# Mixture-of-experts stage of a two-block model on one core: half-array products, transposes and sums put in runs

## Chip, cores and metric

The kernel runs on one core of a Trainium2 chip. The metric is the device time of one execution in microseconds (us), as the median of several runs.

## What is computed

Two model blocks follow each other. The change touches only the last stage of the second block, a hierarchical mixture of experts over 512 tokens of width 1024, in float32:

```python
for g in range(N_GROUPS):
    a = jnp.einsum('td,edf->tef', t, w_gate[g])
    b = jnp.einsum('td,edf->tef', t, w_up[g])
    m = jax.nn.silu(a) * b * combine[:, g, :, None]
    y = y + jnp.einsum('tef,efd->td', m, w_down[g])
```

There are 32 experts in all, each with 256 inner columns; `combine` is zero but for the two best experts of a token's best group. After the stage comes a residual addition and one RMS norm, and the kernel ends.

## The kernel before, in words

A routing step (before the stage) gives each expert a list of at most 64 rows (`CAP`); a list that is longer is finished in a loop at the very end (`further`), which runs zero times here. Each expert is handled on 64 columns of the array, two experts to a pair, so that the 128 partitions of a pair's result are 64 slots of one and 64 of the other.

- **Weights.** An expert's weights come as three pieces of 1 MB (`load_pieces`, issued on the queue of SP, six after each pair), into a ring of 17 tiles (`ew`, `mix`, `cb` in the trace). A tile is loaded again when the products that read it are done; SP waits for that in order.
- **Rows.** The tokens' rows are gathered from memory by POOL (`gather`, eight ahead; tile `hy`), turned on TensorE by four transposes into a bank `pt` (`expert_rows`, line 277), and written to `ex` by VectorE with the norm's gain (line 1906).
- **Inner products** (`expert_inner`, line 1920): 16 matmuls of an expert, 8 contraction steps k for two column halves f. Each uses one half of the array (128x64 weights, 256 columns), the two f side by side. A float32 matmul stands in the trace as two records. The result, in a bank `lin`, goes through ScalarE (Silu, line 1925) and VectorE (line 1926) to `em`; one transpose puts it into `pt`, and VectorE copies it to `emt` (line 1932).
- **Outer products** (`expert_steps`, line 1945): 8 matmuls of a pair, for two halves f of the contraction and two halves i of the 1024 outputs; the two experts of the pair use the two halves of the array side by side. Results stand in two banks `sc`. ScalarE writes their weighted high part and VectorE the low part, both to `ca` (lines 1951, 1952).
- **Sums** (line 1965): eight per pair, for four blocks c of 128 tokens and two halves i. Each is two full-array matmuls of 512 columns with a 0/1 matrix `esel` that puts slots back at their tokens; it lands in one bank, `o` or `bg` by turns, and VectorE adds it to `xrow` (line 1967).

The order around the change: the sums of a pair are a generator (`sums`), and the next pair's `expert_inner` takes a step of it at four places (`beside`): after k = 4, after the products, after the next expert's row transposes, and after the copy to `emt`. So one sum stands at each of eight places of a pair. The list order is only the starting point; a scheduler may move instructions on their engines, save those under `keep_in_program_order`. PSUM has eight banks, by name: two `lin`, two `sc`, two `pt`, one `o`, one `bg`.

```python
some = lambda: next(sums, None)
beside = (some, some, lambda: (rows(e), some()), some)
inner.append(self.expert_inner(ahead.pop(), piece(e), self.slot_rstd[:, e:e + 1], beside))
```

Of the kernel before, what the change touches and what calls it, by code (L numbers as in the profile page):

```python
# [11 lines left out]
F32 = mybir.dt.float32  # L12
# [6 lines left out]
P = 128  # L19
# [86 lines left out]
class Builder:  # L106
    def __init__(self, ctx, tc, a, out):
        self.tc, self.nc, self.a, self.out = tc, tc.nc, a, out
        pool = lambda name, bufs=1, **kw: ctx.enter_context(tc.tile_pool(name=name, bufs=bufs, **kw))
        self.cp = pool("const")  # L110
        self.sm = None
        self.ps = pool("psum", 8, space=bass.MemoryType.PSUM)
        self.uid = 0
        self.background = iter(())
        self.opened, self.seconds = {}, {}
        self.np, self.nw, self.ahead = None, S, 2
        self.turn, self.probs = True, 2
        self.meanwhile = iter(())

    def open(self, name, side="left"):  # L120
# [153 lines left out]

    def transpose(self, out, in_):
        k = in_.shape[0]
        self.nc.tensor.transpose(out, in_, self.ident[:k, :k])  # L277

    def rstd(self, acc, count, ones=None):

# [1626 lines left out]
                                     op=ALU.mult)  # L1907
        return x

    def expert_inner(self, x, pieces, r, beside=None):  # L1910


        nc = self.nc
        beside = beside or [lambda: None] * 4

        ps = self.psum()
        for k in range(KC):
            xk = x[:, P * (k % 4) + CAP * (k // 4):P * (k % 4) + CAP * (k // 4) + CAP]
            for f in range(2):
                nc.tensor.matmul(ps[CAP * f:CAP * f + CAP, :256], xk, pieces(512 * k + 256 * f, 256), start=k == 0,  # L1920
                                 stop=k == KC - 1, tile_position=(0, CAP * f))
            if k == KC // 2:
                beside[0]()
        m = self.t([P, P], F32, "em", 2)
        nc.scalar.activation(out=m, in_=ps[:, :P], func=AF.Silu, scale=r)
        nc.vector.scalar_tensor_tensor(out=m, in0=ps[:, P:2 * P], scalar=r, in1=m, op0=ALU.mult, op1=ALU.mult)
        beside[1]()
        beside[2]()
        pt = self.psum("pt")
        self.transpose(pt[:, :P], m)  # L1930
        mt = self.t([P, P], F32, "emt", 3)
        nc.vector.tensor_copy(mt, pt[:, :P])
        beside[3]()
        return mt

    def expert_steps(self, inner, pieces, y, token, weight):


        nc = self.nc
        n = CAP * len(inner)  # L1940
        o = [self.psum("sc") for _ in range(2)]
        for f in range(2):
            for i in range(2):
                for e, (mt, pc) in enumerate(zip(inner, pieces)):
                    nc.tensor.matmul(o[i][CAP * e:CAP * e + CAP], mt[:, CAP * f:CAP * f + CAP],  # L1945
                                     pc(4096 + 1024 * f + 512 * i, 512), start=f == 0, stop=f == 1,
                                     tile_position=(0, CAP * e))
        ys = []
        for i in range(2):
            yh, yl = y[:n, 2 * i], y[:n, 2 * i + 1]  # L1950
            nc.scalar.activation(out=yh, in_=o[i][:n], func=AF.Copy, scale=weight)
            nc.vector.scalar_tensor_tensor(out=yl, in0=o[i][:n], scalar=weight, in1=yh, op0=ALU.mult,
                                           op1=ALU.subtract)
            ys.append((yh, yl))

        sel = self.t([P, S], FR, "esel", 2)[:n]
        for i in range(2):
            nc.vector.tensor_scalar(out=sel[:, C * i:C * i + C], in0=self.rests[4 + i][:n], scalar1=token, scalar2=None,
                                    op0=ALU.is_equal)
        yield  # L1960
        for c in range(4):
            for i in range(2):
                ps = self.psum(("o", "bg")[i])
                for part in range(2):
                    nc.tensor.matmul(ps, sel[:, c * P:c * P + P], ys[i][part], start=part == 0, stop=part == 1)  # L1965
                acc = self.xrow[4 * i + c]
                nc.vector.tensor_tensor(out=acc, in0=acc, in1=ps, op=ALU.add)
                yield
# [81 lines left out]
    def moe(self):  # L2050
# [19 lines left out]

        def rows(e):

            if e + 1 < 32:
                ahead.append(self.expert_rows(gs[(e + 1) % GATHERED]))
            if e + GATHERED < 32:
                gather(e + GATHERED)

        def piece(e):
            return lambda c, n: self.pieces[3 * e + c // 2048][:, c % 2048:c % 2048 + n]

        for q in range(16):
            inner = []
            for e in (2 * q, 2 * q + 1):
                some = lambda: next(sums, None)
                beside = (some, some, lambda: (rows(e), some()), some)
                inner.append(self.expert_inner(ahead.pop(), piece(e), self.slot_rstd[:, e:e + 1], beside))
            if q == 15:

                self.tc.keep_in_program_order(
                    nc.scalar.activation(out=self.trstd[:, :1], in_=self.eps, func=AF.Sqrt))  # L2090
            sums = self.expert_steps(inner, [piece(2 * q), piece(2 * q + 1)], y, self.pair_token[:, q:q + 1],
                                     self.pair_weight[:, q:q + 1])
            next(sums)
            self.load_pieces(6)
        last = [self.last(c) for c in range(4)]
        for c in range(4):
            whole(itertools.islice(sums, 2))
            next(last[c])
            if c > 0:
                whole(last[c - 1])  # L2100
        whole(last[3])
        self.further(y)
        self.close("moe", "later", "inputs")

    def further(self, y):
# [4 lines left out]
        with self.tc.For_i(0, count, 1) as i:  # L2110
            e = nc.values_load(self.ov[0:1, bass.ds(i, 1)], engines=[mybir.EngineType.SP], min_val=0, max_val=31)
            sl = self.t([P, 4], F32, "osl", 1)
            nc.sync.dma_start(sl, self.table[bass.ds(i, 1)].rearrange("t p c -> p (t c)"))
            oi = self.t([P, 1], I32, "oid", 1)
            nc.vector.tensor_copy(oi, sl[:, 0:1])
            self.gather(g, oi)
            w = [self.t([P, 2048], F32, "ew", RING[0], self.rings[0][0]) for _ in range(3)]
            for k in range(3):
                nc.sync.dma_start(w[k], a["w_moe"][bass.ds(e, 1), :, 2048 * k:2048 * k + 2048].rearrange("e p c -> p (e c)"))
            piece = lambda c, n: w[c // 2048][:, c % 2048:c % 2048 + n]  # L2120
            inner = self.expert_inner(self.expert_rows(g), piece, sl[:, 3:4])
            whole(self.expert_steps([inner], [piece], y, sl[:CAP, 1:2], sl[:CAP, 2:3]))
            for c in range(4):
                whole(self.last(c))

# [216 lines left out]
```

## Time and profile before

| | |
|---|---|
| median of 3 runs (lowest to highest) | 2652.45 us (2650.92 to 2658.2) |
| the profiled execution's own time | 2654.92 us |
| its span, first to last instruction | 2653.1 us |
| the stage: first inner product to the end of the last outer product | 2338.2 to 2629.1 us of the span |
| from there to the end of the span | 24.0 us |
| mean granted TensorE clock | 0.977 of full speed |

Times in the rows are counted from the start of the span. Pair q holds experts 2q and 2q + 1; a pair's length is told from the first inner product of its first expert to that of the next pair.

### The profile page before, as it was taken

How to read it: one execution, taken by the hardware profiler on the slowest of the kernel's cores; microseconds unless marked ns; L12 is line 12 of the kernel's file. 1: busy time of each engine (PE TensorE's matmuls, PEld its weight loads, DVE VectorE, ACT ScalarE, POOL GpSimd, SP SyncE). 2: the span in 40 equal slices, each digit the busy share in tenths (PEclk: the TensorE clock that was granted, in tenths of full speed). 3: DMA queues.
4: the chain of work that ended last, by engine and by line, in shares of the span. 5: the costliest groups of instructions: out<-in, count | busy, mean ns of one | idle time of the engine just before them, and what ended most of it. 6: DMA issues, size and time to landing. Idle time of an engine off the chain costs nothing. (4 is left out here: it accounts for less than half of the span.)

```text
span 2653.1 us, 37574 instructions
## 1 busy us (share of the span) xinstructions
PE 2511.2 (95%) x14286; PEld 2005.6 (76%) x14286; DVE 1711.6 (65%) x2932; ACT 1171.2 (44%) x1971; POOL 432.8 (16%) x448
## 2 busy tenths in 40 slices
PE   7999999999999999989899999999999879989996
PEld 5578776788888888878777988888888768755553
DVE  6657766656667666477777664556788986345554
ACT  6545465555313313355456642335666554301112
POOL 3041121030000000142311200002400540221100
PEclk9999999999999999999999999999999989989998
DMA  7732223342345352252112533233312642689970
GB/s 244 272 132 89 84 80 103 101 152 77 96 124 158 97 182 85 77 168 66 52 40 63 164 102 95 94 100 119 102 49 96 220 133 87 247 319 367 379 316 33
DMA packets 114048, 368.92 MB, mean 139 GB/s; under 512 B 17988, under 2 KB 29648, under 8 KB 101450
## 3 DMA queue, kind: packets, MB, share of 16 engines
q1 hardware_dynamic: 110554, 358.10, 39.8%
q0 software_dynamic: 3312, 8.40, 0.9%
q8 instruction: 114, 1.87, 0.3%
q14 instruction: 68, 0.56, 0.1%
HBM read 356.95 MB, written 13.68 MB: 140 GB/s over the span
## 5 line engine op out<-in xcount | busy, mean ns | idle before, releaser
L198 PE MATMUL lin<-ah,whi 128*128 128x512 f32 (+1 forms) x1504 | 557.2, 371 | 19.0 <-ACT qd L224 9.3
L200 PE MATMUL lin<-al,whi 128*128 128x512 f32 (+1 forms) x1504 | 548.7, 366 | 1.6 <-DVE al L344 1.1
L199 PE MATMUL lin<-ah,wlo 128*128 128x512 f32 (+1 forms) x1504 | 546.1, 364 | 2.8 <-DVE wlo L182 2.8
L181 ACT CAST whi<-wraw 128x1024 fp32r<-128x1024 f32 (+2 forms) x297 | 298.0, 1006 | 313.1 <-PE sc L200 174.4
L182 DVE TENSOR_TENSOR wlo<-wraw,whi 128x1024 fp32r<-128x1024 f32 (+2 forms) x297 | 362.7, 1223 | 85.3 <-ACT whi L181 83.6
L198 PEld LDWEIGHTS lin<-ah,whi 128*128 128x128 f32 x1504 | 287.5, 191 | 69.1 <-ACT qd L224 10.6
L200 PEld LDWEIGHTS lin<-al,whi 128*128 128x128 f32 x1504 | 286.5, 191 | 50.2 <-issue 2.7
L199 PEld LDWEIGHTS lin<-ah,wlo 128*128 128x128 f32 x1504 | 287.3, 191 | 40.7 <-DVE wlo L182 3.3
L323 POOL TENSOR_TENSOR sqacc<-sqacc,sq 128x256 f32<-128x256 f32 (+1 forms) x101 | 128.6, 1279 | 1083.3 <-ACT sq L322 1082.0
L198 PE MATMUL sc<-ah,whi 128*128 128x256 f32 (+1 forms) x696 | 219.6, 316 | 0.0
L199 PE MATMUL sc<-ah,wlo 128*128 128x256 f32 (+1 forms) x696 | 219.3, 315 | 0.0
L200 PE MATMUL sc<-al,whi 128*128 128x256 f32 (+1 forms) x696 | 218.7, 315 | 0.0
L198 PEld LDWEIGHTS sc<-ah,whi 128*128 128x128 f32 x696 | 132.7, 191 | 10.8 <-issue 0.9
L199 PEld LDWEIGHTS sc<-ah,wlo 128*128 128x128 f32 x696 | 132.6, 191 | 10.2 <-DVE wlo L182 0.4
L200 PEld LDWEIGHTS sc<-al,whi 128*128 128x128 f32 x696 | 132.4, 191 | 8.0
L887 DVE SCALAR_TENSOR_TENSOR fv<-lin,vec,fv 128x511 f32<-128x511 f32 x67 | 50.2, 749 | 117.3 <-ACT fv L886 117.3
L1920 PE MATMUL lin<-ew,ex 128*64 128x256 f32 x864 | 115.5, 384 | 0.1
L445 DVE CUSTOM_DVE_ANT_0 mraw<-mraw,crow 128x512 f32<-128x512 f32 x128 | 86.9, 689 | 33.3 <-DMA mraw<-in_w_mod_rows 32.0
L199 PE MATMUL lin<-mh,wlo 128*128 128x512 f32 (+1 forms) x292 | 105.3, 361 | 1.6 <-DVE wlo L182 1.4
L198 PE MATMUL lin<-mh,whi 128*128 128x512 f32 (+1 forms) x292 | 105.3, 361 | 0.0
L200 PE MATMUL lin<-ml,whi 128*128 128x512 f32 (+1 forms) x292 | 104.8, 359 | 0.0
L1920 PEld LDWEIGHTS lin<-ew,ex 128*64 128x64 f32 x864 | 65.2, 136 | 46.3 <-issue 18.3
(636 smaller groups left out, 5346.6 us busy)
## 6 DMA issues: line engine op xcount, KB each, us to landing
ew<-in_w_moe SPq DMA_DIRECT2D x81, 1024.0 KB, 10.8
wraw<-in_w_up SPq DMA_DIRECT2D x88, 512.0 KB, 3.5
wraw<-in_w_in SPq DMA_DIRECT2D x61, 512.0 KB, 3.6
mraw<-in_w_mod SPq DMA_DIRECT2D x48, 512.0 KB, 3.5
mraw<-in_w_mod_rows SPq DMA_DIRECT2D x96, 256.0 KB, 2.8
wraw<-in_w_down SPq DMA_DIRECT2D x48, 448.0 KB, 3.3
wraw<-in_w_out SPq DMA_DIRECT2D x32, 512.0 KB, 3.6
wraw<-in_w_down SPq DMA_DIRECT2D x16, 512.0 KB, 3.6
```

The lines of the kernel that those rows point to most:

```text
L181: nc.scalar.copy(hi[:, :n], raw[:, :n])
L182: nc.vector.tensor_tensor(out=lo[:, :n], in0=raw[:, :n], in1=hi[:, :n], op=ALU.subtract)
L198: mm(out, wh, xh, start=start, stop=False)
L199: mm(out, wl, xh, start=False, stop=False)
L200: mm(out, wh, xl, start=False, stop=stop)
L323: nc.gpsimd.tensor_tensor(out=acc, in0=acc, in1=sq, op=ALU.add)
L445: self.tc.keep_in_program_order(nc.vector.tensor_tensor_reduce(out=x, in0=raw, in1=self.crow[:, i, d], scale=1.0, scalar=0.0, op0=ALU.mult ...
L887: nc.vector.scalar_tensor_tensor(out=v[:, t0 + 1:t1], in0=ps[:, :t1 - t0 - 1], scalar=cw(0), in1=v[:, t0 + 1:t1], op0=ALU.mult, op1=ALU.add)
L1920: nc.tensor.matmul(ps[CAP * f:CAP * f + CAP, :256], xk, pieces(512 * k + 256 * f, 256), start=k == 0, stop=k == KC - 1, tile_position=(0, ...
```

## The change

In pairs, the work on TensorE is put into runs. `expert_inner` now ends with `em`, without transposing it and without steps of other work between. The new `expert_turn` transposes both experts' `em` into one bank `o` and copies both with one VectorE instruction. `expert_steps` is split in `expert_outer` and `expert_sums`. A pair's outer products no longer follow its own inner products: they stand between the two experts of the next pair, with i as the outer loop and f inside. Then come both row transposes for the next pair (`rows` twice), the two inner transposes, and all eight sums in one run, in banks `sc sc lin lin o bg sc sc`. All of these TensorE instructions are kept in program order (`pin`) in the stage. The gathers and the loads are the same, in the same order.

The diff, without the loop `further`, which gets the same calls:

```diff
--- before.py
+++ after.py
@@ -114,7 +114,7 @@
         self.background = iter(())
         self.opened, self.seconds = {}, {}
         self.np, self.nw, self.ahead = None, S, 2
-        self.turn, self.probs = True, 2
+        self.turn, self.probs, self.pinned = True, 2, False
         self.meanwhile = iter(())
 
     def open(self, name, side="left"):
@@ -274,7 +274,12 @@
 
     def transpose(self, out, in_):
         k = in_.shape[0]
-        self.nc.tensor.transpose(out, in_, self.ident[:k, :k])
+        self.pin(self.nc.tensor.transpose(out, in_, self.ident[:k, :k]))
+
+    def pin(self, ins):
+
+        if self.pinned:
+            self.tc.keep_in_program_order(ins)
 
     def rstd(self, acc, count, ones=None):
 
@@ -1907,51 +1912,52 @@
                                      op=ALU.mult)
         return x
 
-    def expert_inner(self, x, pieces, r, beside=None):
-
-
-        nc = self.nc
-        beside = beside or [lambda: None] * 4
+    def expert_inner(self, x, pieces, r):
+
+
+        nc = self.nc
 
         ps = self.psum()
         for k in range(KC):
             xk = x[:, P * (k % 4) + CAP * (k // 4):P * (k % 4) + CAP * (k // 4) + CAP]
             for f in range(2):
-                nc.tensor.matmul(ps[CAP * f:CAP * f + CAP, :256], xk, pieces(512 * k + 256 * f, 256), start=k == 0,
-                                 stop=k == KC - 1, tile_position=(0, CAP * f))
-            if k == KC // 2:
-                beside[0]()
+                self.pin(nc.tensor.matmul(ps[CAP * f:CAP * f + CAP, :256], xk, pieces(512 * k + 256 * f, 256), start=k == 0,
+                                 stop=k == KC - 1, tile_position=(0, CAP * f)))
         m = self.t([P, P], F32, "em", 2)
         nc.scalar.activation(out=m, in_=ps[:, :P], func=AF.Silu, scale=r)
         nc.vector.scalar_tensor_tensor(out=m, in0=ps[:, P:2 * P], scalar=r, in1=m, op0=ALU.mult, op1=ALU.mult)
-        beside[1]()
-        beside[2]()
-        pt = self.psum("pt")
-        self.transpose(pt[:, :P], m)
-        mt = self.t([P, P], F32, "emt", 3)
-        nc.vector.tensor_copy(mt, pt[:, :P])
-        beside[3]()
-        return mt
-
-    def expert_steps(self, inner, pieces, y, token, weight):
-
+        return m
+
+    def expert_turn(self, ms):
+
+        pt = self.psum("o")
+        for i, m in enumerate(ms):
+            self.transpose(pt[:, P * i:P * i + P], m)
+        n = P * len(ms)
+        mt = self.t([P, 2 * P], F32, "emt", 1)
+        self.nc.vector.tensor_copy(mt[:, :n], pt[:, :n])
+        return [mt[:, P * i:P * i + P] for i in range(len(ms))]
+
+    def expert_outer(self, inner, pieces, y, weight):
 
         nc = self.nc
         n = CAP * len(inner)
         o = [self.psum("sc") for _ in range(2)]
-        for f in range(2):
-            for i in range(2):
+        for i in range(2):
+            for f in range(2):
                 for e, (mt, pc) in enumerate(zip(inner, pieces)):
-                    nc.tensor.matmul(o[i][CAP * e:CAP * e + CAP], mt[:, CAP * f:CAP * f + CAP],
+                    self.pin(nc.tensor.matmul(o[i][CAP * e:CAP * e + CAP], mt[:, CAP * f:CAP * f + CAP],
                                      pc(4096 + 1024 * f + 512 * i, 512), start=f == 0, stop=f == 1,
-                                     tile_position=(0, CAP * e))
-        ys = []
+                                     tile_position=(0, CAP * e)))
         for i in range(2):
             yh, yl = y[:n, 2 * i], y[:n, 2 * i + 1]
             nc.scalar.activation(out=yh, in_=o[i][:n], func=AF.Copy, scale=weight)
             nc.vector.scalar_tensor_tensor(out=yl, in0=o[i][:n], scalar=weight, in1=yh, op0=ALU.mult,
                                            op1=ALU.subtract)
-            ys.append((yh, yl))
+
+    def expert_sums(self, y, n, token):
+
+        nc = self.nc
 
         sel = self.t([P, S], FR, "esel", 2)[:n]
         for i in range(2):
@@ -1960,9 +1966,9 @@
         yield
         for c in range(4):
             for i in range(2):
-                ps = self.psum(("o", "bg")[i])
+                ps = self.psum(("sc", "lin", ("o", "bg")[i], "sc")[c])
                 for part in range(2):
-                    nc.tensor.matmul(ps, sel[:, c * P:c * P + P], ys[i][part], start=part == 0, stop=part == 1)
+                    self.pin(nc.tensor.matmul(ps, sel[:, c * P:c * P + P], y[:n, 2 * i + part], start=part == 0, stop=part == 1))
                 acc = self.xrow[4 * i + c]
                 nc.vector.tensor_tensor(out=acc, in0=acc, in1=ps, op=ALU.add)
                 yield
@@ -2070,28 +2076,41 @@
 
         def rows(e):
 
-            if e + 1 < 32:
-                ahead.append(self.expert_rows(gs[(e + 1) % GATHERED]))
-            if e + GATHERED < 32:
-                gather(e + GATHERED)
+            if e < 32:
+                ahead.append(self.expert_rows(gs[e % GATHERED]))
+            if e - 1 + GATHERED < 32:
+                gather(e - 1 + GATHERED)
 
         def piece(e):
             return lambda c, n: self.pieces[3 * e + c // 2048][:, c % 2048:c % 2048 + n]
 
+        def results(q):
+
+            self.expert_outer(inner, [piece(2 * q), piece(2 * q + 1)], y, self.pair_weight[:, q:q + 1])
+            steps = self.expert_sums(y, P, self.pair_token[:, q:q + 1])
+            next(steps)
+            return steps
+
+
+
+        self.pinned = True
+        rows(1)
         for q in range(16):
-            inner = []
+            ms = []
             for e in (2 * q, 2 * q + 1):
-                some = lambda: next(sums, None)
-                beside = (some, some, lambda: (rows(e), some()), some)
-                inner.append(self.expert_inner(ahead.pop(), piece(e), self.slot_rstd[:, e:e + 1], beside))
+                ms.append(self.expert_inner(ahead.pop(0), piece(e), self.slot_rstd[:, e:e + 1]))
+                if e % 2 == 0 and q > 0:
+                    sums = results(q - 1)
             if q == 15:
 
                 self.tc.keep_in_program_order(
                     nc.scalar.activation(out=self.trstd[:, :1], in_=self.eps, func=AF.Sqrt))
-            sums = self.expert_steps(inner, [piece(2 * q), piece(2 * q + 1)], y, self.pair_token[:, q:q + 1],
-                                     self.pair_weight[:, q:q + 1])
-            next(sums)
+            for i in range(2):
+                rows(2 * q + 2 + i)
+            inner = self.expert_turn(ms)
+            whole(sums)
             self.load_pieces(6)
+        sums = results(15)
         last = [self.last(c) for c in range(4)]
         for c in range(4):
             whole(itertools.islice(sums, 2))
@@ -2099,6 +2118,7 @@
             if c > 0:
                 whole(last[c - 1])
         whole(last[3])
+        self.pinned = False
         self.further(y)
         self.close("moe", "later", "inputs")
 
```

In the rows of an instruction order below, each row is a line of the kernel, an operation, the tile written, the tiles read, and a size. Numbers behind names count buffers. First TensorE, at the second expert of a pair in mid-stage. Before:

```order
L1920 MATMUL lin_22671<-ew_22359,ex_22649 64x256 x8
L1920 MATMUL lin_22671<-ew_22361,ex_22649 64x256 x2
L1965 MATMUL o_22682<-ca_21878,esel_22606 128x512 x2
L1920 MATMUL lin_22671<-ew_22361,ex_22649 64x256 x6
L1965 MATMUL bg_22695<-ca_21878,esel_22606 128x512 x2
L277 MATMUL pt_22700<-cmat,hy_14057 128x128 x4
L1965 MATMUL o_22709<-ca_21878,esel_22606 128x512 x2
L277 MATMUL pt_22713<-cmat,em_22692 128x128
L1945 MATMUL sc_22721<-ew_22357,emt_22665 64x512
L1965 MATMUL bg_22717<-ca_21878,esel_22606 128x512 x2
L1945 MATMUL sc_22722<-ew_22357,emt_22665 64x512
```

And now, from the last outer product to the sums of the pair before:

```order
L1949 MATMUL sc_22743<-ew_22458,emt_22676 64x512
L1924 MATMUL lin_22759<-ew_22466,ex_22663 64x256 x8
L1924 MATMUL lin_22759<-ew_22468,ex_22663 64x256 x8
L277 MATMUL pt_22780<-cmat,hy_13837 128x128 x4
L277 MATMUL pt_22790<-cmat,hy_13872 128x128 x4
L277 MATMUL o_22799<-cmat,em_22739 128x128
L277 MATMUL o_22799<-cmat,em_22776 128x128
L1971 MATMUL sc_22804<-ca_21878,esel_22756 128x512 x2
L1971 MATMUL sc_22808<-ca_21878,esel_22756 128x512 x2
L1971 MATMUL lin_22812<-ca_21878,esel_22756 128x512 x2
L1971 MATMUL lin_22816<-ca_21878,esel_22756 128x512 x2
L1971 MATMUL o_22820<-ca_21878,esel_22756 128x512 x2
```

The sums stood one at a time between runs of inner products (line 1920), transposes (line 277) and outer products (line 1945). Now 32 inner and 8 outer products come without a full-array instruction between, and the 10 transposes and 16 matmuls of the sums in one run behind them.

Then VectorE, for the same place. Before:

```order
L1926 SCALAR_TENSOR_TENSOR em_22771<-lin_22750,srs_21269,em_22771 128x128
L1967 TENSOR_TENSOR xrow_21602<-xrow_21602,bg_22774 128x512
L1906 TENSOR_TENSOR ex_22778<-pt_22779,vec 128x512
L1967 TENSOR_TENSOR xrow_21434<-xrow_21434,o_22788 128x512
L1932 COPY emt_22794<-pt_22792 128x128
L1967 TENSOR_TENSOR xrow_21609<-xrow_21609,bg_22796 128x512
L1967 TENSOR_TENSOR xrow_21441<-xrow_21441,o_22811 128x512
L1926 SCALAR_TENSOR_TENSOR em_22821<-lin_22800,srs_21269,em_22821 128x128
L1967 TENSOR_TENSOR xrow_21616<-xrow_21616,bg_22824 128x512
L1906 TENSOR_TENSOR ex_22828<-pt_22829,vec 128x512
```

And now:

```order
L1928 SCALAR_TENSOR_TENSOR em_22739<-lin_22722,srs_21269,em_22739 128x128
L1955 SCALAR_TENSOR_TENSOR ca_21878<-sc_22742,pw_21268,ca_21878 128x512
L1955 SCALAR_TENSOR_TENSOR ca_21878<-sc_22743,pw_21268,ca_21878 128x512
L1928 SCALAR_TENSOR_TENSOR em_22776<-lin_22759,srs_21269,em_22776 128x128
L1911 TENSOR_TENSOR ex_22779<-pt_22780,vec 128x512
L1911 TENSOR_TENSOR ex_22789<-pt_22790,vec 128x512
L1938 COPY emt_22802<-o_22799 128x256
L1973 TENSOR_TENSOR xrow_21427<-xrow_21427,sc_22804 128x512
L1973 TENSOR_TENSOR xrow_21602<-xrow_21602,sc_22808 128x512
L1973 TENSOR_TENSOR xrow_21434<-xrow_21434,lin_22812 128x512
```

The adds to `xrow` stood between the steps that make `em`, `ex` and `emt`. Now they follow in a row behind these; `emt` is copied once for both experts, and behind both `ex`.

## Rows read from the trace of the kernel before

**Rows 1.** Windows: stage, a pair, tail; window, length, busy us, clock, DMA share, GB/s.

```profile
core 0: us, PE busy (x) PEld busy (x) DVE busy (x) ACT busy (x) POOL busy (x), PEclk, DMA share, GB/s
...
2494.43:2512.23 17.80, 17.80 (x109) 9.43 (x106) 9.38 (x18) 2.11 (x4) 1.99 (x2) 1.00 0.94 376
2338.20:2629.10 290.90, 285.51 (x1672) 149.41 (x1672) 143.68 (x277) 35.83 (x66) 25.14 (x26) 1.00 0.76 301
2629.10:2653.10 24.00, 6.08 (x17) 2.46 (x16) 14.88 (x29) 9.46 (x27) 5.93 (x7) 0.68 0.23 89
```

**Rows 2.** Waits of PE in the stage: total us, times, longest us.

```profile
PE pt L277 <- DVE em L1926: 3.6, 4, 1.0
```

**Rows 3.** Timeline of PE, pair 9: start us, us, what, records.

```profile
2497.55 0.73 PE L1965 MATMUL o<-ca,esel 128*128 128x512 f32 x2
2498.21 1.51 PE L1920 MATMUL lin<-ew,ex 128*64 128x256 f32 x12
2499.66 0.74 PE L1965 MATMUL bg<-ca,esel 128*128 128x512 f32 x2
2500.23 0.60 PE L277 MATMUL pt<-cmat,hy 128*128 128x128 f32 x4
2500.59 0.71 PE L1965 MATMUL o<-ca,esel 128*128 128x512 f32 x2
2501.13 0.27 PE L277 MATMUL pt<-cmat,em 128*128 128x128 f32 x1
...
2507.93 1.07 PE L1945 MATMUL sc<-ew,emt 128*64 128x512 f32 x2
```

**Rows 4.** Timeline of PE, first and last pairs.

```profile
2338.20 5.83 PE L1920 MATMUL lin<-ew,ex 128*64 128x256 f32 x50
...
2351.66 0.38 PE L1920 MATMUL lin<-ew,ex 128*64 128x256 f32 x1
...
2565.97 0.60 PE L1920 MATMUL lin<-ew,ex 128*64 128x256 f32 x2
...
2589.29 1.95 PE L1920 MATMUL lin<-ew,ex 128*64 128x256 f32 x16
...
2595.56 0.63 PE L1965 MATMUL bg<-ca,esel 128*128 128x512 f32 x2
2596.03 0.27 PE L277 MATMUL pt<-cmat,em 128*128 128x128 f32 x1
...
2609.96 1.95 PE L1920 MATMUL lin<-ew,ex 128*64 128x256 f32 x16
2611.84 0.51 PE L1965 MATMUL bg<-ca,esel 128*128 128x512 f32 x1
...
2625.61 3.65 PE L1945 MATMUL sc<-ew,emt 128*64 128x512 f32 x12 [0.39 <-DVE emt L1932]
2629.19 0.49 PE L1965 MATMUL o<-ca,esel 128*128 128x512 f32 x1
```

**Rows 5.** Timeline, all engines, behind the inner products of expert 29.

```profile
2603.42 0.37 ACT L1925 ACTIVATE em<-lin,srs 128x128 f32<-128x128 f32 x1 [7.95 <-PE lin L1920]
...
2604.22 0.33 PE L277 MATMUL pt<-cmat,em 128*128 128x128 f32 x1 [0.86 <-DVE em L1926]
```

**Rows 6.** Timeline of DVE, two instructions in a row, pair 6.

```profile
2454.25 0.68 DVE L1906 TENSOR_TENSOR ex<-pt,vec 128x512 f32<-128x512 f32 x1
2454.85 0.68 DVE L1967 TENSOR_TENSOR xrow<-xrow,o 128x512 f32<-128x512 f32 x1
```

**Rows 7.** Windows of the loads in the stage, columns as in rows 1.

```profile
2338.00:2356.00 18.00, 16.88 (x112) 8.85 (x112) 5.27 (x14) 3.39 (x5) 4.42 (x5) 1.00 0.98 295
2356.00:2374.00 18.00, 18.00 (x110) 9.58 (x112) 9.60 (x19) 2.11 (x4) 1.99 (x2) 1.00 0.88 346
2390.00:2435.00 45.00, 45.00 (x276) 24.13 (x273) 23.26 (x45) 4.60 (x9) 4.98 (x5) 1.00 1.01 417
2338.00:2575.00 237.00, 235.88 (x1411) 125.25 (x1409) 121.06 (x236) 29.09 (x54) 25.34 (x26) 1.00 0.93 368
```

**Rows 8.** Waits of SP's queue, 2250 to 2653 us: total us, times, longest us.

```profile
SPq L1977 <- PE sc L1945: 105.6, 21, 12.3
```

More of the change, by code (lines that the diff above doesn't have):

```diff
@@ L2120, in further @@
             piece = lambda c, n: w[c // 2048][:, c % 2048:c % 2048 + n]
-            inner = self.expert_inner(self.expert_rows(g), piece, sl[:, 3:4])
-            whole(self.expert_steps([inner], [piece], y, sl[:CAP, 1:2], sl[:CAP, 2:3]))
+            inner = self.expert_turn([self.expert_inner(self.expert_rows(g), piece, sl[:, 3:4])])
+            self.expert_outer(inner, [piece], y, sl[:CAP, 2:3])
+            whole(self.expert_sums(y, CAP, sl[:CAP, 1:2]))
             for c in range(4):
```

## Prediction

> **What bounds the kernel now.** I read the windows of the stage first, then the waits of TensorE in it, then its timeline, then the windows of the loads.
>
> The stage takes 290.9 us, and TensorE counts as busy for 285.5 of them at the full clock; the 24.0 us behind it are VectorE's and ScalarE's [rows 1]. TensorE's longest kind of wait in the stage, for `em`, sums to 3.6 us [rows 2]. So TensorE is the bound, and what the stage can win lies in how its busy time is used. VectorE is at work for 9.38 us of a pair's 17.80 [rows 1], and the loads have slack: SP's queue stood 105.6 us waiting for outer products to free tiles [rows 8].
>
> The pairs are not alike [rows 4]. Pair 0 takes 13.5 us (2338.20 to 2351.66), pairs 1 to 12 together 214.3, or 17.86 each (to 2565.97), pair 13 23.3, pair 14 20.7 (to 2609.96), and pair 15 up to the end of its outer products 19.2 (to 2629.19). That makes the 291.
>
> What the work itself needs is read from runs that nothing cuts. A run of 16 records of inner products takes 1.88 us up to what follows (2609.96 to 2611.84) [rows 4], one of 12 records 1.45 (2498.21 to 2499.66) [rows 3]. The 4 records between them are one step k: 0.43 us. An expert's eight steps are then 3.44 us, and 1.45 - 3 x 0.43 = 0.16 us is the price of coming from full-array work and going back to it. A sum inside a full-array run takes 0.47 us (2595.56 to 2596.03) [rows 4], a lone one between inner products 0.66 (2497.55 to 2498.21) [rows 3]: 0.19 more. One change to the full array and back thus costs 0.16 + 0.19 = 0.35 us. Four transposes and a sum take 0.90 us (2500.23 to 2501.13) [rows 3], so a transpose is (0.90 - 0.47) / 4 = 0.11. A pair's outer products in one run take 3.58 us from 2625.61 to 2629.19 [rows 4], or 3.43 without one change.
>
> A pair without changes is therefore 2 x 3.44 + 3.43 + 10 x 0.11 + 8 x 0.47 = 15.2 us. The order before has five changes there and back in a steady pair, 1.75 us, which gives 16.9. The last 0.9 us to 17.86 goes where one half of the array works alone: at 2507.93 one expert's outer product (two records, 1.07 us) runs with nothing in the other half, because a sum stands ahead of its partner [rows 3].
>
> **The change, part by part.**
>
> *Order on TensorE.* A pair now has one change there and back: 15.2 + 0.35 = 15.5 us. No row shows outer products directly behind inner ones in both halves; this may cost nothing, as nothing changes in how the array is split, or at most the 0.16 us of a change. I take nothing, since it is nearest to the products that follow each other inside a run; the bound is 0.16 x 2 x 15 = 5 us.
>
> *The chain to `emt`.* Behind the last inner product come Silu, `em`, and the inner transposes; at expert 29 TensorE stood idle for 0.86 us for it [rows 5]. Now eight row transposes (8 x 0.11 = 0.88) and the first expert's own transpose stand there, so it is covered; in pair 15, which has no row transposes, 0.86 of idle time takes their place, and the sum is the same. The copy to `emt` waits behind two `ex` on VectorE, but its reader, the outer products, comes after 3.8 us of sums and 3.4 of inner products. I cost it at nothing; should it come late, the sums in bank `o` are what waits, since the inner transposes hold that bank.
>
> *Sums and adds.* Two `ex`, the copy and eight adds are queued on VectorE in a row. Independent instructions of 512 columns start 0.60 us apart there (2454.25 to 2454.85), each lasting 0.68 [rows 6]. With `em` done at time 0, the copy counted as long as an `ex`, the first add starts at 1.8 us and ends at 2.5. TensorE needs its bank again for the seventh sum, at about 0.3 + 6 x 0.47 = 3.1. The next inner products need the first `lin`, whose add is the third: 1.8 + 2 x 0.60 + 0.68 = 3.7, against 0.3 + 3.8 = 4.1. The first `sc` of the next outer products is free at 1.8 + 6 x 0.60 + 0.68 = 6.1, against 7.5. All are covered, the tightest by 0.4 us. At 0.68 a step instead of 0.60 it is still 0.2. Fewer copies (16 for 32) are off the path.
>
> *First and last pair.* Pair 0 has no outer products and no sums: 6.9 us of inner products, 0.86 for the chain and 0.68 for the `ex` that the next pair needs, about 8.6 with one change. Behind pair 15 the outer products stand alone: 3.4. The tail has the same instructions on the same engines, with more banks for its sums; I keep 24.0, plus or minus 1.
>
> *Gathers and loads.* POOL's and SP's orders are the same. A gather starts when its row transposes are done, now two close together. The piece for the outer products is held half a pair longer, and the loads queue behind it. The loads moved 368 GB/s x 237 us = 87 MB in the stage, up to 2575 [rows 7]. At the 417 GB/s that they hold when not waiting they need 209 us, to 2547; the last expert's inner products would now begin near 2571. So a lead of 24 us covers the longer hold and the stops that the ring makes.
> The Trainium skill, "DMA: Bandwidth & Descriptors", section "Where 436 GB/s comes from", says that the memory side binds transfers from HBM at about 358 GB/s a core. Here 45 us on end ran at 417 [rows 7], so the measurement decides, and the forecast is not cut by it.
>
> *The sum.* 8.6 + 15 x 15.5 + 3.4 = 244.5 us in place of 290.9: 46.4 less. Against the profiled execution, 2654.92 - 46.4 = 2608.5; that execution was 2.5 us over the median of the runs, so the median comes to **2606 us**. Of the gain, 28 us are in pairs 1 to 12 (12 x 2.36), 13 in pairs 13 and 14, 5 in pair 0. The uncertain terms: 5 us for the joins of inner and outer products, 3 us if each pair waits 0.2 us for a bank, 1 for the tail; the other way, about 3 if sums in a long run are quicker than 0.47, and 1 for the tail. So this case's own range is 2602 to 2614.
>
> **The rivals.**
>
> *The loads become the bound, still faster (0.12).* A pair carries 6.3 MB of weights and mostly 0.5 MB of gathers, 6.8 in all, which at 15.5 us asks for 440 GB/s; the rows never show that, so the lead shrinks from pair to pair. For it: in the second window of the stage, with gathers among the loads, they ran at 346 GB/s [rows 7]. At that rate 87 MB need 252 us and end at 2590; some 12 us of products and sums follow: 2602 in place of 2583, so 2606 + 19 = 2625. Against it: 417 in the longest stretch. Between 346 and about 373, where the lead is used up, the time lies between 2606 and 2625.
> By the rule of the Trainium skill named above ("DMA: Bandwidth & Descriptors"), 358 GB/s, the estimate is 87 / 0.358 = 243 us, loads to 2581, and about 2616 us; the trace does not bear it out.
>
> *The adds set the pace (0.08).* If VectorE's adds don't overlap as assumed and every sum waits at 0.68 us for its bank, a pair has 8 x 0.21 = 1.7 us more, 25 in all: 2631. For it: in the run of sums the adds have no other work to hide behind. Against it: six banks, and VectorE at work for 9.4 us of 15.5.
> The Trainium skill, "TensorEngine Tiling (Array Packing)", section "PSUM Bottleneck", says the same: packing the array speeds up TensorE and not the emptying of PSUM, which may become the limit. The rows show the emptying at 60% of the new pair, so I leave this rule a small chance.
>
> *The runs don't pay (0.04).* If what I put down to changes and half-used arrays is in the products themselves, a steady pair stays at 17.8, and only pairs 0, 13 and 14 become regular: 8.6 + 15 x 17.8 + 3.4 = 279, 12 us less, 2640.
>
> *Slower: the loads starve TensorE (0.03).* The stage's first window moved 295 GB/s at a DMA share of 0.98, gathers among the weights [rows 7]. If denser pairs and the longer-held outer pieces keep the loads in that state, 87 MB need 295 us, to 2633; with 12 us behind it the stage ends 16 us later than before: 2668. It decides below 87 MB in 279 us, 312 GB/s. Against it: that window lies behind the routing's small stores and the burst of the first gathers, and the rate rises from window to window.
>
> **How the numbers follow.** The forecast has 0.73. A measurement of this kernel tells about 0.3% (8 us) from no change. The forecast, both milder rivals and the runs that don't pay (2640) are all faster by more than that, together 0.97; I take something off for what I have not seen: faster 0.94, same 0.03, slower 0.03. The range is the forecast's own, 2602 to 2614, which I trust to nine in ten (0.66), carried on to 2623 to take in most of the two milder rivals (0.14): 2601 to 2623.
>
> **What would show it.** Right: steady pairs of 15.5 us; the 16 records of the sums in about 3.8 us behind ten transposes; outer products behind inner ones without a gap; the last outer product's end near 2583; VectorE's share of a pair near 60%. Wrong: idle time of TensorE ahead of `lin` or `sc` with an add as releaser (the adds); idle time with a DMA as releaser, growing in later pairs (the loads); pairs near 17.8 with TensorE busy throughout (the runs don't pay). A tail that is longer than 25 us would make the prediction wrong in a place where I expect nothing.

## The result, and the profile after

The changed kernel took **2605.98 us** (median; 2605.8 to 2606.64) against 2654.16 of the kernel before in the same session: a ratio of 0.9821 (95% interval 0.9806 to 0.9837). Forecast: 2606. Its profiled execution took 2606.64 us, with a span of 2604.8. Line numbers moved a little: inner products are now L1924, outer products L1949, sums L1971, adds L1973, `em` L1928, `ex` L1911, `emt` L1938.

Windows of the changed kernel: the stage, pair 8, 45 us of the loads, the end of the loads, the tail (columns as in [rows 1]):

```profile
2336.14:2581.54 245.40, 243.44 (x1672) 151.61 (x1672) 138.72 (x262) 35.83 (x66) 25.04 (x26) 1.00 0.89 357
2468.57:2484.05 15.48, 15.48 (x107) 9.65 (x106) 9.04 (x18) 2.11 (x4) 2.00 (x2) 1.00 1.02 414
2390.00:2435.00 45.00, 45.00 (x314) 27.80 (x313) 25.67 (x50) 6.33 (x12) 5.12 (x6) 1.00 1.01 414
2550.00:2560.00 10.00, 10.00 (x69) 6.15 (x66) 4.86 (x10) 1.82 (x4) 0.00 (x0) 1.00 0.33 137
2581.54:2604.80 23.26, 4.61 (x18) 2.86 (x16) 13.21 (x28) 9.28 (x26) 6.21 (x7) 0.71 0.24 91
```

The stage has 245.4 us where it had 290.9 [rows 1]. In both, and in the table below, it is counted from the first inner product to 0.43 us after the start of the last outer record; the record itself lasts 0.59 us in the trace, so the end of the last outer product is 0.16 us later throughout. The tail fell from 24.0 to 23.3. TensorE is busy for all of the pair, VectorE for 9.04 of 15.48 us (58%).

TensorE's timeline in that pair, which answers to [rows 3] (start us, us, what, records; the sums in `o` and `bg` are left out):

```profile
2468.59 3.67 PE L1924 MATMUL lin<-ew,ex 128*64 128x256 f32 x32
2472.10 3.60 PE L1949 MATMUL sc<-ew,emt 128*64 128x512 f32 x16
2475.53 3.62 PE L1924 MATMUL lin<-ew,ex 128*64 128x256 f32 x32
2479.08 1.09 PE L277 MATMUL pt<-cmat,hy 128*128 128x128 f32 x8
2480.01 0.38 PE L277 MATMUL o<-cmat,em 128*128 128x128 f32 x2
2480.15 1.18 PE L1971 MATMUL sc<-ca,esel 128*128 128x512 f32 x4
2481.17 1.10 PE L1971 MATMUL lin<-ca,esel 128*128 128x512 f32 x4
...
2483.04 1.10 PE L1971 MATMUL sc<-ca,esel 128*128 128x512 f32 x4
2484.07 0.44 PE L1924 MATMUL lin<-ew,ex 128*64 128x256 f32 x2
```

Start to start, the outer products take 3.43 us (2472.10 to 2475.53), and they follow the inner ones without a gap. The run of 16 records of the sums takes 3.92 us from 2480.15 to the next inner product. All pairs 1 to 14 are alike: 15.47 or 15.48 us, where pairs 13 and 14 had 23.3 and 20.7 before [rows 4].

VectorE behind the same pair's last inner product:

```profile
2479.60 0.35 DVE L1928 SCALAR_TENSOR_TENSOR em<-lin,srs,em 128x128 f32<-128x128 f32 x1 [2.36 <-ACT em L1927]
2479.87 1.28 DVE L1911 TENSOR_TENSOR ex<-pt,vec 128x512 f32<-128x512 f32 x2
2481.06 0.42 DVE L1938 COPY emt<-o 128x256 f32<-128x256 f32 x1
2481.39 1.28 DVE L1973 TENSOR_TENSOR xrow<-xrow,sc 128x512 f32<-128x512 f32 x2
2482.59 1.28 DVE L1973 TENSOR_TENSOR xrow<-xrow,lin 128x512 f32<-128x512 f32 x2
2483.78 0.68 DVE L1973 TENSOR_TENSOR xrow<-xrow,o 128x512 f32<-128x512 f32 x1
```

The two `ex` start 0.60 us apart and so do the adds; the copy is followed by the first add after 0.33. `em` is ready at 2479.95 and its reader, the second inner transpose, comes at 2480.12: the chain that cost 0.86 us before [rows 5] is covered.

What TensorE still waits for in the stage and the start of the tail (total us, times, longest us), in place of [rows 2]:

```profile
PE sc L1949 <- DVE xrow L1973: 1.1, 1, 1.1
PE sc L1971 <- DVE xrow L1973: 0.9, 1, 0.9
PE o L277 <- DVE em L1928: 0.6, 1, 0.6
```

No matmul waits for a DMA (weight loads name one five times, 1.5 us in all), and none of these waits is in a steady pair: they stand behind pair 15's inner products (a fourth, 0.3 us in pair 0, has no releaser). The first one is new, and I had not foreseen it:

```profile
2578.05 3.65 PE L1949 MATMUL sc<-ew,emt 128*64 128x512 f32 x16 [1.10 <-DVE xrow L1973]
2581.64 0.73 PE L1971 MATMUL sc<-ca,esel 128*128 128x512 f32 x2
2583.24 1.07 PE L1971 MATMUL sc<-ca,esel 128*128 128x512 f32 x2 [0.87 <-DVE xrow L1973]
```

The last pair's outer products have no inner products of a next pair in front of them. They want `sc` directly behind a run of sums that ended in `sc`, and wait 1.10 us for the adds.

### The profile page after: what moved, and what is told of

Its sections match the earlier page's. It is cut to its first block, busy times and chain, and to the rows that moved or that the text cites. A ratio compares the mean times of both kernels' runs of the same rounds, so it can differ in the third digit from the quotient of the medians.

```text
span 2604.8 us, 37537 instructions
## 1 busy us (share of the span) xinstructions
PE 2461.1 (94%) x14286; PEld 2002.3 (77%) x14286; DVE 1707.2 (66%) x2916; ACT 1169.6 (45%) x1971; POOL 434.0 (17%) x448
## 3 DMA queue, kind: packets, MB, share of 16 engines
q8 instruction: 113, 1.85, 0.3%
## 5 line engine op out<-in xcount | busy, mean ns | idle before, releaser
L1924 PE MATMUL lin<-ew,ex 128*64 128x256 f32 x864 | 98.7, 381 | 0.3 <-issue 0.3
L891 ACT ACTIVATE fv<-lin,vec 128x512 f32<-128x512 f32 x67 | 52.1, 778 | 102.1 <-PE lin L200 85.6
## 6 DMA issues: line engine op xcount, KB each, us to landing
ew<-in_w_moe SPq DMA_DIRECT2D x81, 1024.0 KB, 16.6
```

The lines of the kernel that those rows point to most:

```text
L891: nc.scalar.activation(out=v[:, t0:t1], in_=ps, func=AF.Identity, scale=cw(1), bias=self.col("conv_b", 44 * l + f))
L1924: self.pin(nc.tensor.matmul(ps[CAP * f:CAP * f + CAP, :256], xk, pieces(512 * k + 256 * f, 256), start=k == 0, stop=k == KC - 1, tile_posi ...
```

## The experiments

All of them change only the stage. The work ahead of it is the same in every kernel, yet the stage began anywhere from 2332.8 to 2341.7 us in the twelve profiled executions (2338.2 before, 2336.1 after). I therefore compare pairs inside the stage; the medians are given beside them (that of before was 2653.4 to 2655.7 in the other sessions).

| kernel | pair, us | stage, us | median, us |
|---|---|---|---|
| before | 17.80 | 290.9 | 2654.16 |
| changed | 15.48 | 245.4 | 2605.98 |
| 1 before, kept order | 17.36 | 278.4 | 2643.06 |
| 2 the same, copy covered | 16.76 | 268.2 | 2628.98 |
| 3 changed, free order | 15.48, last four 17.4 to 20.1 | 264.9 | 2625.58 |
| 4 sums in two runs | 15.93 | 251.7 | 2613.76 |
| 5 sums in two banks | 18.80 | 296.1 | 2658.62 |
| 6 sums in four banks | 15.99 | 252.7 | 2610.24 |
| 7 one half after the other | 17.25 | 274.9 | 2638.15 |
| 8 chain not covered | 16.29 | 259.0 | 2619.61 |
| 9 other banks for the last run | 15.48 | 244.3 | 2609.16 |
| 10 two copies | 15.48 | 246.5 | 2605.78 |

(Pair: the median of pairs 1 to 14. Pair and stage are from one profiled execution of each kernel, the medians from 2 to 10 executions, which lie up to 7.3 us apart.)

**1. The order before, kept.** The kernel before, with `pin` around the stage's matmuls and transposes:

```diff
-        self.nc.tensor.transpose(out, in_, self.ident[:k, :k])
+        self.pin(self.nc.tensor.transpose(out, in_, self.ident[:k, :k]))
```

> The kernel before, with TensorE's instructions of the stage kept in program order and nothing else changed: sums still stand one at a time between products, but in every pair the eight outer products are together, both halves at work, so that no lone half is left and pairs 13 and 14 are like the others. A pair then has four changes there and back between half-array and full-array instructions, against one in the changed kernel and five before. Theory (a change there and back costs 0.35 us, and a lone half what it takes alone): steady pairs of 15.2 + 4 x 0.35 = 16.6 us, up to 0.5 more if the outer products wait for the copy to emt, which only one sum now covers; in all about 16 us over the changed kernel, 2620 to 2630 us. Rival 1 (only the regular order counts, changes cost nothing): 15.2 to 15.5 a pair, 2606 to 2610. Rival 2 (the gain is only in the runs, an order that is kept is worth nothing): 17.9 a pair, near 2650.

17.36 us a pair, 0.76 over the 16.6, and 2643 in all: rival 1 falls, rival 2's 17.9 is not reached either, and the theory's size was off (0.26 over its 16.6 + 0.5 in each pair; pair 0, with 18.1 us, adds to the total). The slow pairs 13 and 14 are gone, so they came from the scheduler's order. Where are the 0.76? The timeline behind the sums, with TensorE's weight loads (PEld):

```profile
2460.04 3.95 PE L1950 MATMUL sc<-ew,emt 128*64 128x512 f32 x15
2460.43 0.28 DVE L1937 COPY emt<-pt 128x128 f32<-128x128 f32 x1
...
2460.77 0.32 PEld L1950 LDWEIGHTS sc<-ew,emt 128*64 128x64 f32 x4 [0.54 <-DVE emt L1937]
...
2463.52 0.59 PE L1925 MATMUL lin<-ew,ex 128*64 128x256 f32 x2
...
2463.83 0.59 PE L1950 MATMUL sc<-ew,emt 128*64 128x512 f32 x1
```

The outer products of the second expert (the other half of the array) wait 0.73 us for the copy to `emt`; the first expert's begin at 2460.04. TensorE counts as busy throughout, and its list of waits is silent; only the list of its weight loads (PEld) names the copy, 0.54 us in this pair. The lag stays to the end: one half goes on to inner products at 2463.52 while the other still works on outer ones.

**2. The same, with the copy covered.** One sum of each expert moves behind the inner transpose:

```diff
-                beside = (some, some, lambda: (rows(e), some()), some)
+                beside = (some, some, lambda: rows(e), lambda: (some(), some()))
```

> The kernel before in a kept order, as in the experiment before_kept, but with the third sum of each expert moved from between row and inner transposes to behind the inner transposes, so that two sums instead of one cover the copy to emt. The number of changes between half-array and full-array instructions stays at four there and back. Theory (in before_kept a pair of 17.36 us was 15.2 + 4 x 0.35 = 16.6 and a wait of one half of the array for emt, 0.73 us, that no idle time shows since the other half worked): that wait goes, pairs of 16.6 to 16.7 us, unless the chain to em, now with one sum less in front, shows up to 0.3 more an expert. Rival (17.36 is what four changes cost, 0.54 each): 17.3 to 17.4 a pair.

16.76 us. The second half now starts 0.13 us behind the first:

```profile
2463.46 0.64 PE L1950 MATMUL sc<-ew,emt 128*64 128x512 f32 x1
...
2463.59 0.64 PE L1950 MATMUL sc<-mix,emt 128*64 128x512 f32 x1
```

The pair lost 0.60 us, which is the lag that went (0.73 - 0.13). Without the 0.13 that is left, three more changes there and back than in the changed kernel cost 16.63 - 15.48 = 1.15 us, 0.38 each, so the price of a change holds and the rival's 0.54 falls. The single records say the same: around the lone sum at 2459.17 the step from the last inner product is 0.10 us longer than between inner products, that between the sum's two records 0.10 longer than inside a run, that back to the inner products 0.09 and the next one 0.05, or 0.34 to 0.35 together. The Trainium skill, "TensorEngine Tiling (Array Packing)", section "Key Properties", says that a change of the tiling mode drains TensorE. The trace agrees as far as each change costs time, 0.34 to 0.38 us there and back; whether it is a drain, no run here shows.

From the start of pair 1 to that of pair 15 the kernel before took 258.3 us, experiment 1 242.8, this one 235.1 and the changed kernel 216.8. So of the 41.5 us gained there, 15.5 come with the kept order, 7.7 with covering the copy, and 18 with the runs.

**3. The changed kernel without the kept order** (`self.pinned = True` removed).

> The changed kernel without the kept order: the scheduler moves some transposes, mostly one of the row transposes ahead of the inner products of a pair's first expert, so that the stage has 11 more changes there and back between half-array and full-array instructions; everything else stays. Theory: 11 x 0.35 = 3.9 us more, 2608 to 2612. Rival (keeping the order is what most of the gain rests on, since the scheduler's order also makes waits): 2615 or more. Rival (a change costs nothing): no difference, 2606.

2625.6: my theory falls, and the time lies where the first rival put it. But "most of the gain" is too much: without the kept order 28.6 of the 48.2 us are still gained, so 19.6 rest on it. Pairs 1 to 10 are as in the changed kernel. Pair 11 has 17.4 us and pairs 12 to 14 19.7 to 20.1; the last gathers are issued in pair 10. From there on the scheduler splits the run of sums, as this timeline shows:

```profile
2548.57 1.95 PE L1924 MATMUL lin<-mix,ex 128*64 128x256 f32 x16
2550.45 0.73 PE L1971 MATMUL lin<-ca,esel 128*128 128x512 f32 x2
2551.96 0.50 PE L1971 MATMUL lin<-ca,esel 128*128 128x512 f32 x1 [0.78 <-DVE xrow L1973]
2552.39 1.95 PE L1924 MATMUL lin<-mix,ex 128*64 128x256 f32 x16
2554.27 0.49 PE L1971 MATMUL lin<-ca,esel 128*128 128x512 f32 x1
2555.14 0.55 PE L277 MATMUL pt<-cmat,hy 128*128 128x128 f32 x3 [0.37 <-DVE ex L1911]
```

Sums stand between inner products again, transposes between sums, and there are waits for adds and `ex`. In the kernel before the slow pairs 13 and 14 also lay behind the last gather (2536.7). That the end of the gathers is what turns the scheduler's order was not tested.

**4. One more change per pair.** The second four sums stand behind the next pair's first inner products. The main line of the edit is below; besides, `whole(sums)` stands ahead of `results` and behind the loop, and the banks of the eight sums are now `sc sc bg lin` and `o lin bg o`, so this experiment changes banks too.

```diff
-            whole(sums)
+            whole(itertools.islice(sums, 4))
```

> The changed kernel with the eight sums in two runs of four: the second run stands behind the inner products of the next pair's first expert, ahead of the outer products. One more change there and back per pair (14 in the stage), no work added. Theory: pairs of 15.48 + 0.35 = 15.83 us, 5 us more in all, 2609 to 2613. Rival (a change there and back costs nothing and the lone halves are all of the gain): 15.48 a pair, 2606.

15.93 us, 0.45 more (forecast 0.35), and 2613.8 in all, just over the forecast. About 0.1 of the 0.45 is probably the reuse of bank `o` by the run's last sum, between whose two records 0.335 us pass, as against 0.235 inside a run; that was not tested. The rest fits the change. The rival falls.

**5. Two banks for all sums.**

```diff
-                ps = self.psum(("sc", "lin", ("o", "bg")[i], "sc")[c])
+                ps = self.psum(("o", "bg")[i])
```

> The changed kernel with the eight sums of a run only in the banks o and bg, as before the change. Theory: a sum has to wait for the add of the sum two places ahead, and adds are 0.60 to 0.68 us apart with the add's wait behind each sum, so the run is paced by the adds or by sum plus add in turn: about 1.5 to 3 us more in each of 15 pairs, 22 to 45 us in all, 2630 to 2650; TensorE then shows waits for o and bg with an add as releaser. Rival (the adds keep up, banks don't matter): under 0.3 us a pair, 2606 to 2610.

3.32 us a pair more and 2658.6 in all, beyond the forecast: this would have made the changed kernel slower than the one before (a ratio of 1.0019, 95% interval 1.0009 to 1.0028). PE and DVE in a steady pair:

```profile
2434.77 0.38 PE L277 MATMUL o<-cmat,em 128*128 128x128 f32 x2
2435.82 0.42 DVE L1938 COPY emt<-o 128x256 f32<-128x256 f32 x1
...
2436.38 0.70 PE L1971 MATMUL o<-ca,esel 128*128 128x512 f32 x2 [1.23 <-DVE emt L1938]
...
2436.92 0.63 PE L1971 MATMUL bg<-ca,esel 128*128 128x512 f32 x2
2437.12 0.69 DVE L1973 TENSOR_TENSOR xrow<-xrow,o 128x512 f32<-128x512 f32 x1 [0.88 <-PE o L1971]
...
2437.86 0.73 PE L1971 MATMUL o<-ca,esel 128*128 128x512 f32 x2 [0.31 <-DVE xrow L1973]
```

The first sum waits 1.23 us, since bank `o` still holds the inner transposes until the copy has read them; I had counted only the adds. Then two sums take 1.5 us (2436.38 to 2437.86) where a run without waits takes 0.94, as each waits for the add two places ahead: up to the next inner product at 2442.15 the 8 sums take 5.8 us instead of 3.9. The run also begins 1.61 us after the first inner transpose instead of 0.14. Both together, 1.85 and 1.47, are the 3.3. The Trainium skill, "TensorEngine Tiling (Array Packing)", section "PSUM Bottleneck", says that packing the array speeds up TensorE and not the emptying of PSUM, which may become the bottleneck. Here the work is not packed, the sums are full-array matmuls; their emptying is the limit with two banks (5.8 us) and not with six (3.9).

**6. Four banks.**

```diff
-                ps = self.psum(("sc", "lin", ("o", "bg")[i], "sc")[c])
+                ps = self.psum(("lin", "sc", "lin", "sc")[c])
```

> The changed kernel with the eight sums of a run in four banks instead of six (lin lin sc sc lin lin sc sc); o holds the inner transposes alone. Theory: the first add begins 1.24 us after the first sum (in the changed kernel), the adds follow 0.60 us apart and last 0.68, the sums 0.47; the fifth sum waits for the first add, due at 1.92, and comes at 1.96, and from there the adds set the pace: the last sum ends 0.3 to 0.4 us later, and the next inner products wait another 0.1 for the add of the fifth sum: 0.4 to 0.6 us a pair, 6 to 9 us in all, 2611 to 2616. Rival (what made two banks cost 3.3 us a pair was mostly that bank o was held by the inner transposes; four free banks are enough): under 0.2 us a pair, 2605.5 to 2609.

15.99 us, 0.51 more, inside the forecast of a pair; the 2610.2 in all are 0.8 under its 2611. TensorE's timeline of the run:

```profile
2450.51 1.18 PE L1971 MATMUL lin<-ca,esel 128*128 128x512 f32 x4
2451.53 1.10 PE L1971 MATMUL sc<-ca,esel 128*128 128x512 f32 x4
2452.49 1.33 PE L1971 MATMUL lin<-ca,esel 128*128 128x512 f32 x4
2453.68 1.33 PE L1971 MATMUL sc<-ca,esel 128*128 128x512 f32 x4
2454.94 0.44 PE L1924 MATMUL lin<-mix,ex 128*64 128x256 f32 x2
```

The first two blocks of four records follow at 1.0 us; the third takes 1.19 and the fourth 1.26 to the next inner product, the pace of the adds (0.60 each). The rival falls: four banks are not enough to hide the adds, and six are.

**7. One half of the array after the other** (`e` as the outer loop of the outer products).

> The changed kernel with a pair's outer products expert by expert: the four of the first (one half of the array), then the four of the second (the other half), the same instructions otherwise. Theory (the two halves only work side by side as far as instructions for both stand next to each other in the order): the 3.43 us of a pair's outer products become up to 6.9; the last product of one half may overlap the first of the other (0.86 us at two joins), so 1.7 to 3.4 us more in each of 15 pairs and behind the last, 27 to 55 us in all, 2633 to 2661. Rival (each half takes its next instruction on its own, however far down the order it stands): no difference, 2606.

1.77 us a pair, at the low end. The timelines of PE and of its weight loads (PEld) show why not 3.4:

```profile
2424.08 4.08 PE L1949 MATMUL sc<-ew,emt 128*64 128x512 f32 x13
2425.80 0.19 PEld L1949 LDWEIGHTS sc<-ew,emt 128*64 128x64 f32 x3 [0.29 <-issue]
...
2427.58 0.65 PE L1924 MATMUL lin<-ew,ex 128*64 128x256 f32 x2
...
2428.86 0.59 PE L1949 MATMUL sc<-ew,emt 128*64 128x512 f32 x1
```

The merged first row holds two series of records, 0.43 us apart in each. The first expert's eight run from 2424.08, the second expert's eight from 2425.80: the second half starts 1.72 us after the first, beside the fifth of the first half's eight records, where it would have started after 3.43 us if it waited for all of them. That delay is nearly all of the 1.77. Four records of the next inner products already run in the free half (2427.58 and, in the rows left out, 2428.43), but they gain nothing: from 2429.29, where both halves are at inner products, these take 3.55 us as in the changed kernel. So each half goes on by itself, but only a little ahead of the order: both times the half that is free starts past three records that wait for the other half; the rival, unlimited lead, falls.

**8. The inner transposes ahead of the row transposes.**

> The changed kernel with the two inner transposes ahead of the eight row transposes instead of behind them. Theory (the row transposes cover the chain from the last inner product over Silu and em): TensorE stands idle for 0.86 us less the first expert's transpose, 0.11, so 0.75 us more in pairs 1 to 14 and none in pair 15, 11 us in all, 2614 to 2620; the idle time has em as its releaser. Rival (the chain is covered anyway, or the copy to emt, now ahead of both ex on VectorE, lets the adds start earlier and gives it back): within 3 us of 2606.

0.81 us a pair, 2619.6. The wait is where it should be:

```profile
2420.82 0.33 PE L277 MATMUL o<-cmat,em 128*128 128x128 f32 x1
2421.74 0.33 PE L277 MATMUL o<-cmat,em 128*128 128x128 f32 x1 [0.60 <-DVE em L1928]
2421.91 1.04 PE L277 MATMUL pt<-cmat,hy 128*128 128x128 f32 x8
```

From the first inner transpose to the second 0.92 us pass instead of 0.11, 0.60 of them named as a wait for `em`.

**9. Other banks for the last run of sums** (`sc sc lin lin o bg lin lin` there).

> The changed kernel with one run of sums, the last that stands in the stage, put into other banks: its seventh and eighth sum go to lin instead of sc, so that the outer products of the last pair, which follow it directly, find sc free. Theory: the 1.1 us that those products waited for sc goes; 1.1 us less, 2604.5 to 2605.5. Rival (the wait comes back in the tail, which waits for the same adds on VectorE): no difference, 2605.8 to 2606.6.

The 1.10 us wait is gone, and from the first inner product to the end of the span 267.7 us pass instead of 268.7. The time of the whole, 2609.16 (2606.05 to 2612.28), does not tell the two apart; the start of the stage moves by more than that. So the times bear out neither forecast. By the one trace of each this is the better version, by 1 us.

**10. Two banks and two copies for the inner transposes.**

> The changed kernel with the two inner transposes in two banks (o and bg) and one copy for each, as before the change, instead of one bank and one copy for both. Theory (VectorE works for about 57% of a pair, and the slack of the adds against their banks takes a copy of 0.3 us): at most 0.2 us a pair, 2605.5 to 2609. Rival (the one copy is a part of the gain, since two copies delay all eight adds and the sums wait for banks): 0.3 us or more a pair, 2610.5 or more.

15.48 us a pair, as in the changed kernel. The single copy is no part of the gain.

## Why the prediction was right

- *The steady pair.* Forecast 15.5, measured 15.48. The price of a change between half-array and full-array instructions, 0.35 us, taken from a few rows, came out as 0.34 to 0.38 (experiment 2) and as at most 0.45 (4), where 0.35 is left if the bank cost the other 0.1. The joins of inner and outer products cost nothing, as chosen between 0 and 5 us.
- *The pair before.* The 0.9 us that I put down to lone halves fits what is left (17.80 - 15.48 - 4 x 0.35 = 0.92), but no run took only the lone halves out of the kernel before. Experiment 1 shows that such a loss can also come from a wait of one half, which TensorE's list of waits does not have.
- *The chain and the banks.* Both covered, by 0.17 us for `em`; the first add began 1.44 us after `em`, where I had 1.8, so the banks had more room than forecast. Experiments 8, 5 and 6 show what each is worth uncovered: 0.81, 3.3 and 0.5 us a pair.
- *Pair 15, mis-sized.* "Behind pair 15 the outer products stand alone: 3.4": they took 3.43, but 1.10 us late. I had checked the bank `sc` for the steady pair, with inner products between, and not for this one. The stage came out 0.9 over the 244.5.
- *The tail* was 0.7 shorter, within the 1 allowed, and the stage began 2.1 us earlier than in the profile before, which the change has no part in. So the profiled execution was 1.9 under the 2608.5 (0.9 - 0.7 - 2.1). I had then taken off 2.5 for the median, and here the profiled execution was only 0.7 above it. That these errors all but cancel, and the median comes out at 2606, is luck.
- *The loads.* They did not bind: 414 GB/s for 45 us, and done about 2553, 15 us ahead of the last expert's inner products at 2568.4. I had expected a lead of 24. By the limit that the Trainium skill states ("DMA: Bandwidth & Descriptors", section "Where 436 GB/s comes from"), about 358 GB/s, an estimate for the 87 MB is 243 us, to 2579, and the lead would have been used up; this trace, with 414 GB/s, again does not bear it out.
- *The rivals.* Adds that set the pace exist, with two or four banks and not with six. That the runs don't pay is refuted by experiments 2 and 4. Pairs that became merely regular gave 15.5 of the 41.5 us of pairs 1 to 14 (experiment 1), and 23 with the copy covered as well (2).

## What to carry to other kernels

Where half-array and full-array matmuls alternate, count the changes: here each there and back cost about 0.35 us. Collecting the full-array ones in a run only pays if their results have banks enough for the pace of the engine that empties them, so work out when each bank comes free, for the last iteration too, where the cover is missing. And look at each half's own first record: a half that waits while the other works is not in TensorE's list of waits, only in that of its weight loads.

## What was not expected of the hardware

A wait of TensorE was followed by a stretch at half the clock. In experiment 1, pair 0 took 18.1 us. Its first expert's `em` stood on VectorE behind an instruction that waited for a DMA, TensorE was idle for 3.62 us, and soon after it had resumed the granted clock was at 0.50, which is 1.2 GHz. The windows of that idle time and of the slow stretch:

```profile
2345.70:2349.30 3.60, 0.05 (x1) 0.00 (x0) 1.47 (x4) 1.20 (x2) 1.00 (x1) 1.00 0.90 234
2351.00:2354.00 3.00, 3.00 (x16) 1.70 (x14) 0.00 (x0) 0.00 (x0) 0.00 (x0) 0.50 1.03 430
```

In the 3 us of the second window the inner products' records of one half stood 0.427 us apart instead of 0.216. That the idle time was the cause I did not test. Pair 0 is no steady number either. Behind a 4.5 us wait ahead of the stage the clock was at 0.56 up to the first inner product in the changed kernel and at 0.50 in experiment 5; over the next 5.1 us it was at 1.00 in the first and at 0.68 in the second, whose pair 0 took 10.2 us instead of 8.6. My 8.6 for pair 0 was therefore partly luck.
